# The first stage of a conv/attention block kernel: row sums of squares on TensorE, scale and shift in one turn, and another order of steps

## The chip, the cores and the metric

The kernel runs on one core of a Trainium2 chip. The metric is the device time of one execution in microseconds (us); lower is better. Every time below comes from the timed runs of the kernel before or from the trace of one profiled execution of it.

## What is computed

Two layers of a small diffusion transformer work on 256 latent tokens (`x`) and 256 context tokens (`ctx`) of width 1024, in float32. The first stage, which the change concerns, is the beginning of layer 0:

```
mod = (silu(c) @ mod_w[i] + mod_b[i]).reshape(bsz, 3, 3, 1, D_MODEL)
modc = (silu(c_ctx) @ mod_w[i] + mod_b[i]).reshape(3, 3, D_MODEL)
h = rms(x) * g * (1 + scale) + shift       # scale = mod[:,0,1], shift = mod[:,0,0]
gte, up = split(h @ w13, 2)                # FFN_HIDDEN = 2816 columns each
x = x + 0.5 * gate * ((silu(gte) * up) @ w2)
```

`rms(x)` divides each token by the root of the mean of its squares over the 1024 features. `c` (for x) and `c_ctx` (for ctx) give two sets of scale and shift. After this feed-forward part come a short convolution, a second feed-forward, grouped attention and two more feed-forwards; they are not changed.

## The kernel before, in words

**Layout.** Features lie on the 128 partitions: `x` is 128 x 8 x 512, feature tile k (0 to 7) by 512 tokens, the latent 256 first (s = 0), then the context 256 (s = 1). Weights come from HBM as float32; ScalarE rounds each to a high part (`wh`, L108), VectorE forms the rest (`wl`, L109), and a product is three matmuls: high by high, low by high, high by low. Each of these moves 512 columns. Plain float32 matmuls (those on `ones`, `ident`, `rowsum`, `sccol`) are issued as two passes each, so the trace counts two instructions for one call.

**Constants.** Five small loads go out on ScalarE's DMA queue through `cload` (L72): `ccol`, `modb`, `normg`, `ident`, `rowsum`. The four loads of `x`, 512 KB each, go out on SP's queue (L81). All later loads of the first stage go out on SP's queue in the order of the step list. In the program the DMAs of these two queues take eight completion semaphores in turn, and an issue waits until the DMA that used its semaphore eight places earlier has landed.

**The row sums.** `square_add` (L254 to L263) squares each tile of `x` on ScalarE and adds it to `acc` on VectorE. `rms_sum` (L265 to L280) then multiplies `acc` with a column of ones: for 128 tokens one matmul with `acc` as the weights and one moving column (L270), four in all; then the root on ScalarE and the reciprocal on VectorE. `rms_all` (L285 to L292) spreads the result over all partitions with `ident` (L288), and `first_inv` copies it to SBUF (`ris`, L947).

**Scale and shift.** A quarter q covers two feature tiles. `mod_load` (L907) loads 1 MB of modulation weights for the scale (ch = 1) or the shift (ch = 0). `mod_pe` (L912) multiplies them with the padded silu(c) in `sccol`, 32 columns of weights in four column groups of the array at once (L920, eight matmuls), and copies the 256 sums from PSUM to `row` (L925, ScalarE). `mod_turn` (L928) turns the row into columns with `rowsum` (L932, two matmuls) and adds the bias (L937, VectorE). Scale and shift of one quarter are two `mod_pe` and two `mod_turn`.

**The order.** Inside a `manual_schedule` block the instructions of TensorE, VectorE, ScalarE and SP are issued in the order in which the program writes them. After `fill(WARM)` (39 matmuls of `ones` by `ones` that no result uses, L891) and the sums, the string `FIRST_STEPS` is gone through: L loads modulation weights, R loads FFN weights, P is `mod_pe`, X is `first_inv`, U is `scale_q` (x times g times `ris`, L957), T is `mod_turn`, W splits a quarter of the FFN weights, F is `fill(FILL)` (5 matmuls), N is `norm_one` (the normalised tile and its low part, L967 to L981), h, w, l are the three kinds of product for one FFN column block i, quarter q and tile j, M all six of them for both tiles, S the last load. The three column blocks i = 0, 1, 2, four quarters, two tiles, three kinds and two halves (gate and up) make 144 matmuls of 512 columns (all L994). The next block, i = 3, begins at L137. After that the kernel is the same in both versions.

## Time and profile before

| | |
|---|---|
| time, median of 3 runs | 1556.71 us (1556.7 to 1556.72) |
| the profiled execution | 1558.75 us |
| its span in the trace | 1557.0 us |
| TensorE (PE) busy | 1545.5 us, 99% of the span |
| VectorE (DVE) busy | 1284.5 us, 82% |
| ScalarE (ACT) busy | 781.9 us, 50% |
| granted TensorE clock, mean | 0.999 |

In the profile PE is the matmul side of TensorE, PEld its weight loads, SPq and ACTq the DMA issues of those queues. A row of the timeline has the start, the length, the engine, the line, the operation, the tiles (out<-in), the shape, how many instructions are merged in it, and in brackets how long the engine was idle before it and what ended that. Neighbouring matmuls overlap, so the distance between their starts, and not their length, is what one costs in a row of many.

### The profile page before, as it was taken

How to read it: one execution, taken by the hardware profiler on the slowest of the kernel's cores; microseconds unless marked ns; L12 is line 12 of the kernel's file. 1: busy time of each engine (PE TensorE's matmuls, PEld its weight loads, DVE VectorE, ACT ScalarE, POOL GpSimd, SP SyncE). 2: the span in 40 equal slices, each digit the busy share in tenths (PEclk: the TensorE clock that was granted, in tenths of full speed). 3: DMA queues.
4: the chain of work that ended last, by engine and by line, in shares of the span. 5: the costliest groups of instructions: out<-in, count | busy, mean ns of one | idle time of the engine just before them, and what ended most of it. 6: DMA issues, size and time to landing. Idle time of an engine off the chain costs nothing.

```text
span 1557.0 us, 26280 instructions
## 1 busy us (share of the span) xinstructions
PE 1545.5 (99%) x10252; PEld 1416.9 (91%) x10252; DVE 1284.5 (82%) x2003; ACT 781.9 (50%) x1297; POOL 221.8 (14%) x187
## 2 busy tenths in 40 slices
PE   9999999999999999999999999999999999999999
PEld 7898998998888899989999899989999899998888
DVE  5789799799987489978979888968978888898676
ACT  5642553544322366436446476436446455774553
POOL 0012212200000012032032012022042002300000
PEclk9999999999999999999999999999999999999999
DMA  9557477475565424655656634655767843266562
GB/s 368 197 167 197 115 186 203 111 199 166 187 204 178 115 62 121 207 142 146 199 149 153 205 77 123 203 156 133 220 183 169 263 158 122 92 237 221 170 196 75
DMA packets 88254, 263.53 MB, mean 169 GB/s; under 512 B 10817, under 2 KB 12609, under 8 KB 88129
## 3 DMA queue, kind: packets, MB, share of 16 engines
q1 hardware_dynamic: 69408, 230.72, 45.7%
q0 software_dynamic: 16128, 29.37, 11.3%
q10 hardware_dynamic: 2592, 1.76, 0.4%
q8 instruction: 80, 1.31, 0.3%
q14 instruction: 46, 0.37, 0.1%
HBM read 259.45 MB, written 1.05 MB: 167 GB/s over the span
## 4 chain that ended last, share of the span: by engine, by line
PE 96%; DVE 2%; ACT 1%; DMA 1%; issue 0%; POOL 0%; ACTq 0%; DVEq 0%; POOLq 0%
PE py L138 9%; PE py L137 9%; PE py L139 9%; PE p L137 7%; PE p L139 7%; PE p L138 7%; PE q L137 5%; PE q L139 5%; PE q L138 5%; PE py L145 2%; PE pu L145 2%; PE pg L145 2%; PE py L147 1%; PE pg L147 1%; PE pu L147 1%; PE pv L137 1%
## 5 line engine op out<-in xcount | busy, mean ns | idle before, releaser
L108 ACT ACTIVATE wh<-wr 128x1024 fp32r<-128x1024 f32 (+2 forms) x446 | 394.7, 913 | 338.0 <-PE py L138 128.1
L109 DVE TENSOR_TENSOR wl<-wr,wh 128x1024 fp32r<-128x1024 f32 (+2 forms) x446 | 456.5, 1048 | 84.3 <-ACT wh L108 64.7
L178 DVE CUSTOM_DVE_ANT_0 junk<-wr,scbc,modb 128x1024 bf16<-128x1024 f32 x213 | 274.5, 1289 | 8.7 <-DMA wr<-in_modT 6.9
L138 PE MATMUL py<-gl,wh 128*128 128x512 f32 (+1 forms) x570 | 213.4, 374 | 0.0
L137 PE MATMUL py<-gh,wh 128*128 128x512 f32 (+1 forms) x570 | 213.3, 374 | 0.0
L139 PE MATMUL py<-gh,wl 128*128 128x512 f32 (+1 forms) x570 | 212.9, 373 | 0.0
L699 POOL TENSOR_SCALAR wr<-wr 128x512 f32<-128x512 f32 x56 | 101.3, 1809 | 542.4 <-DMA wr<-in_w 292.2
L562 DVE SCALAR_TENSOR_TENSOR x<-py,mod,x 128x256 f32<-128x256 f32 x213 | 94.2, 478 | 66.5 <-PE py L139 55.0
L137 PE MATMUL p<-th,wh 128*128 128x256 f32 x448 | 126.8, 283 | 0.0
L139 PE MATMUL p<-th,wl 128*128 128x256 f32 x448 | 126.8, 283 | 0.0
L138 PE MATMUL p<-tl,wh 128*128 128x256 f32 x448 | 126.8, 283 | 0.0
L139 PEld LDWEIGHTS py<-gh,wl 128*128 128x128 f32 x570 | 107.3, 188 | 19.3
L137 PEld LDWEIGHTS py<-gh,wh 128*128 128x128 f32 x570 | 107.4, 188 | 18.3
L138 PEld LDWEIGHTS py<-gl,wh 128*128 128x128 f32 x570 | 107.4, 188 | 18.0
L115 POOL DMA_DIRECT2D w4l<-in_w x56 | 54.1, 966 | 445.2 <-ACT w4l L114 423.6
L137 PE MATMUL q<-bh,wh 128*128 128x256 f32 x320 | 90.8, 284 | 0.8 <-ACT wh L108 0.8
L139 PE MATMUL q<-bh,wl 128*128 128x256 f32 x320 | 90.8, 284 | 0.0
L138 PE MATMUL q<-bl,wh 128*128 128x256 f32 x320 | 90.5, 283 | 0.0
L138 PEld LDWEIGHTS p<-tl,wh 128*128 128x128 f32 x448 | 86.0, 192 | 0.3
L137 PEld LDWEIGHTS p<-th,wh 128*128 128x128 f32 x448 | 86.0, 192 | 0.3
L139 PEld LDWEIGHTS p<-th,wl 128*128 128x128 f32 x448 | 86.0, 192 | 0.0
L759 ACT ACTIVATE sg<-sg 128x512 f32<-128x512 f32 x56 | 35.4, 632 | 90.9 <-DVE sg L758 90.6
(303 smaller groups left out, 4060.4 us busy)
## 6 DMA issues: line engine op xcount, KB each, us to landing
wr<-in_w SPq DMA_DIRECT2D x120, 512.0 KB, 4.8
wr<-in_modT SPq DMA_DIRECT2D x117, 512.0 KB, 4.7
wr<-in_w2b SPq DMA_DIRECT2D x64, 448.0 KB, 4.0
wr<-in_w2a SPq DMA_DIRECT2D x32, 512.0 KB, 4.5
wr<-in_w SPq DMA_DIRECT2D x56, 256.0 KB, 3.9
wr<-in_w POOLq DMA_DIRECT2D x56, 256.0 KB, 5.9
w4l<-in_w POOLq DMA_DIRECT2D x56, 256.0 KB, 6.0
pm<-in_mod SPq DMA_DIRECT2D x16, 512.0 KB, 10.2
```

The lines of the kernel that those rows point to most:

```text
L108: nc.scalar.activation(out=hi, in_=src, func=AF.Copy)
L109: return nc.vector.tensor_tensor(out=lo, in0=src, in1=hi.bitcast(F32), op=ALU.subtract)
L115: nc.gpsimd.dma_start(out=lo, in_=src, accum_op=ALU.add)
L137: nc.tensor.matmul(ps, wh, mh, start=first, stop=False, **kw)
L138: nc.tensor.matmul(ps, wh, ml, start=False, stop=False, **kw)
L139: nc.tensor.matmul(ps, wl, mh, start=False, stop=last, **kw)
L145: nc.tensor.matmul(ps, w[0], m[2], start=first and n == 0, stop=False)
L147: nc.tensor.matmul(ps[:, :S], w[1], m[0], start=False, stop=last and n == len(ms) - 1)
L178: nc.vector.tensor_tensor_reduce(out=junk, in0=raw, in1=scbc[:, v, :], scale=0.5 if ch in (2, 8) else 1.0, scalar=modb[:, l, col : col + 1 ...
L562: ins = nc.vector.scalar_tensor_tensor(out=x[:, m, s * S : s * S + S], in0=ps[:, o : o + S], scalar=g[:, m, s : s + 1], in1=x[:, m, s * S ...
L699: nc.gpsimd.tensor_scalar(out=r1[:, :T2], in0=r2[:, :T2], scalar1=-1.0, scalar2=None, op0=ALU.mult)
L759: nc.scalar.activation(out=self.sg, in_=self.sg, func=AF.Silu)
```

## The change

1. **Sums.** `square_add` is no longer used in this stage. `first_sums` squares the even tiles of `x` on ScalarE and the odd ones on VectorE, and multiplies each squared tile at once with a column of ones, four matmuls per tile, which add up in PSUM over the eight tiles: 32 matmuls in place of 4. `first_inv` does root, reciprocal and spreading for all four token blocks together.
2. **Turn.** The shift's matmuls add into the same PSUM rows as the scale's (`sccol` is padded so that the two land in different rows of a group of 32), so that one copy and one `mod_turn` (two matmuls with four columns, then two additions) serve both.
3. **Fills.** `WARM` goes from 39 to 30; F takes its count from the step list, which has F6 ahead of the spreading, F12 ahead of the first shift product, F4 ahead of the first turn, and F5 where F was. Together 57 in place of 44.
4. **Order.** In the later quarters, other products stand between P and T: `w100 w101 h200` in the first, `h011 w011 l011` in the second, `h211 w211 l211` in the third. Some M steps are written out as h, w, l. W of block 2's first half is cut into H (ScalarE) and D (VectorE), set apart.
5. **Second copy of a normalised tile.** `norm_one` makes it on VectorE for (q, j) = (0,0), (2,0), (3,0) and on ScalarE for the rest; before, VectorE did all of quarter 0 and every j = 0.
6. **One constant load.** The five small arrays are packed into `first` (128 x 340) and loaded by one DMA.

```diff
-WARM = 39
-FILL = 5
+WARM = 30
 FIRST_STEPS = (
-    "L10 L00 R00 R10 P10 X U0 L11 P00 L01 T10 T00 W00 N00 W01 N01 F h000 w000 l000 R20 W10 "
-    "W11 h001 w001 h100 h101 l001 l100 l101 U1 P11 L12 P01 L02 T11 T01 w100 w101 N10 N11 W20 "
-    "W21 U2 M01 R01 R11 P12 L13 P02 L03 T12 T02 M11 R21 N20 N21 W02 W03 M20 W12 W13 U3 M21 "
-    "P13 P03 T13 T03 W22 W23 M02 N30 N31 M12 M22 M03 M13 M23 S"
+    "L10 L00 R00 R10 F6 X U0 P10 L11 F12 P00 L01 F4 T0 W00 N00 W01 N01 F5 h000 w000 l000 R20 W10 "
+    "W11 h001 w001 h100 h101 l001 l100 l101 U1 H20 H21 P11 L12 P01 L02 w100 w101 h200 T1 D20 D21 "
+    "N10 N11 h201 l200 l201 w200 w201 U2 h010 w010 l010 R01 R11 P12 L13 P02 L03 h011 w011 l011 T2 "
+    "M11 R21 N20 N21 W02 W03 W12 W13 U3 h210 w210 l210 P13 P03 h211 w211 l211 T3 W22 W23 M02 "
+    "N30 N31 M12 M22 M03 M13 M23 S"
 )
-    ccol = cload("ccol", [P, KT, 2])
+    first = cload("first", [P, CUTS[-1]])
+    ccol, modb, normg, ident, rowsum = (first[:, a:b] for a, b in zip(CUTS, CUTS[1:]))
...
-    for k in range(KT):
-        square_add(k, 0, T2)
...
             nc.tensor.matmul(
-                pr[g : g + 32, :S], sccol[:, k, :], raws[k // 4][:, o : o + S],
-                start=(k < 4), stop=(k >= 4), tile_position=(0, g),
-            )
+                pr[g : g + 32, :S], sccol[:, k, c : c + 32], raws[k // 4][:, o : o + S],
+                start=(ch == 1 and k < 4), stop=(ch == 0 and k >= 4), tile_position=(0, g),
+            )
...
+    def first_sums():
+
+        pq = psmall("ss")
+        for k in range(KT):
+            sq = tp.tile([P, T2], F32, name=nm("sq"), tag="sg" if k % 2 else "gm", bufs=3)
+            if k % 2:
+                nc.vector.tensor_tensor(out=sq, in0=x[:, k, :], in1=x[:, k, :], op=ALU.mult)
+            else:
+                nc.scalar.activation(out=sq, in_=x[:, k, :], func=AF.Square)
+            for i in range(4):
+                nc.tensor.matmul(
+                    pq[:, S + i : S + i + 1], sq[:, i * P : i * P + P], ones[:, 0:1],
+                    start=(k, i) == (0, 0), stop=(k, i) == (KT - 1, 3), skip_group_check=True,
+                )
+        return pq
...
-            if q == 0 or j == 0:
+            if (q, j) in ((0, 0), (2, 0), (3, 0)):
...
         fill(WARM)
-        sums = [rms_sum(s) for s in range(2)]
+        pqs = first_sums()
```

More of the change, by code (lines that the diff above doesn't have):

```diff
@@ L27 @@
 EARLY = 4
+CUTS = (0, 16, 160, 208, 336, 340)
 HEADS = 8
@@ L75, in cload @@
         return t
-    ccol = cload("ccol", [P, KT, 2])
+    first = cload("first", [P, CUTS[-1]])
+    ccol, modb, normg, ident, rowsum = (first[:, a:b] for a, b in zip(CUTS, CUTS[1:]))
+    ccol = ccol.rearrange("p (k v) -> p k v", v=2)
+    modb = modb.rearrange("p (l c) -> p l c", l=2)
+    normg = normg.rearrange("p (l j k) -> p l j k", l=2, j=3)
     x = act.tile([P, KT, T2], F32, name="x", tag="x")
@@ L81, in hybrid_kernel @@
         nc.sync.dma_start(x[:, 2 * q : 2 * q + 2, :], a["xT"][:, 2 * q : 2 * q + 2, :])
-    modb = cload("modb", [P, 2, 72])
-    normg = cload("normg", [P, 2, 3, KT])
-    ident = cload("ident", [P, P])
     ones = const.tile([P, P], F32, name="ones", tag="ones")
@@ L92, in hybrid_kernel @@
     )
-    sccol = const.tile([P, KT, 32], F32, name="sccol", tag="sccol")
+    sccol = const.tile([P, KT, 34], F32, name="sccol", tag="sccol")
     nc.vector.memset(sccol, 0.0)
-    nc.scalar.activation(out=sccol[:, :, :2], in_=ccol, func=AF.Silu)
-    rowsum = cload("rowsum", [P, 2])
+    nc.scalar.activation(out=sccol[:, :, 2:4], in_=ccol, func=AF.Silu)
     scbc = mp.tile([P, 2, D], F32, name="scbc", tag="scbc", bufs=1)
@@ L500, in second @@
             def second():
-                z.ri = tp.tile([P, S], F32, name=nm("ris"), tag="ris0", bufs=1)
+                z.ri = tp.tile([P, T2], F32, name=nm("ris"), tag="ris", bufs=1)[:, :S]
                 nc.scalar.copy(z.ri, rms_all(*box["ri"]))
@@ L915, in mod_pe @@
         raws = rows[ch, q]
-        pr = psum("pr") if (ch, q) == (1, 0) else psmall("pr")
+        if ch:
+            rows[q] = psum("pr") if q == 0 else psmall("pr")
+        pr = rows[q]
+        c = 2 if ch else 0
         for k in range(KT):
@@ L920, in mod_pe, with mod_turn @@
             nc.tensor.matmul(
-                pr[g : g + 32, :S], sccol[:, k, :], raws[k // 4][:, o : o + S],
-                start=(k < 4), stop=(k >= 4), tile_position=(0, g),
-            )
+                pr[g : g + 32, :S], sccol[:, k, c : c + 32], raws[k // 4][:, o : o + S],
+                start=(ch == 1 and k < 4), stop=(ch == 0 and k >= 4), tile_position=(0, g),
+            )
+    def mod_turn(q):
+        pr = rows[q]
         row = tp.tile([P, T2], F32, name=nm("row"), tag="gm", bufs=3)
         nc.scalar.copy(row[:, :S], pr[:, :S])
-        rows[ch, q] = pr, row
-    def mod_turn(ch, q):
-        pr, row = rows[ch, q]
         for j in range(2):
             nc.tensor.matmul(
-                pr[:, S + 2 * j : S + 2 * j + 2], row[:, j * P : j * P + P], rowsum,
+                pr[:, S + 4 * j : S + 4 * j + 4], row[:, j * P : j * P + P], rowsum,
                 start=True, stop=True,
@@ L936, in mod_turn, with first_inv @@
         k2 = slice(2 * q, 2 * q + 2)
-        nc.vector.tensor_tensor(
-            out=(A00 if ch else B00)[:, k2, :],
-            in0=pr[:, S : S + 4].rearrange("p (k v) -> p k v", v=2),
-            in1=both(sb1[:, k2] if ch else modb[:, 0, k2]),
-            op=ALU.add,
-        )
-    def first_inv():
+        turned = pr[:, S : S + 8].rearrange("p (k c v) -> p k c v", k=2, c=2)
+        for ch in (1, 0):
+            nc.vector.tensor_tensor(
+                out=(A00 if ch else B00)[:, k2, :], in0=turned[:, :, 1 - ch, :],
+                in1=both(sb1[:, k2] if ch else modb[:, 0, k2]), op=ALU.add,
+            )
[13 more added lines that the diff above has]
+        return pq
+    def first_inv(pq):
+        rs = tp.tile([P, 4], F32, name=nm("rs"), tag="rs4", bufs=1)
+        nc.scalar.activation(
+            out=rs, in_=pq[:, S : S + 4], func=AF.Sqrt, scale=1.0 / D, bias=eps_t
+        )
+        ri = tp.tile([P, 4], F32, name=nm("ri"), tag="ri4", bufs=1)
+        nc.vector.reciprocal(ri, rs)
+        t = tp.tile([P, T2], F32, name=nm("ris"), tag="ris", bufs=1)
         for s in range(2):
-            ris.append(tp.tile([P, S], F32, name=nm("ris"), tag=f"ris{s}", bufs=1))
-            nc.scalar.copy(ris[s], rms_all(*sums[s]))
+            ris.append(t[:, s * S : s * S + S])
+            nc.scalar.copy(ris[s], rms_all(psmall("ri") if s else pq, ri[:, 2 * s : 2 * s + 2]))
     def raw_of(k, s):
@@ L1023, in first_raw, with first_w, put @@
         ws[i] = lambda o: tuple(t[:, o % T2 : o % T2 + P] for t in cut[i][o // T2])
-    def first_w(i, p):
-        j = (1, 0, 3, 2)[p]
-        o = j % 2 * T2
-        ins = split(*cut[i][j], raws[i, j // 2][:, o : o + T2])
-        rows[f"W{i}"] = ins.ins
+    def first_w(part):
+        def put(i, p):
+            j = (1, 0, 3, 2)[p]
+            o = j % 2 * T2
+            hi, lo = cut[i][j]
+            raw = raws[i, j // 2][:, o : o + T2]
+            if part != "D":
+                nc.scalar.activation(out=hi, in_=raw, func=AF.Copy)
+            if part != "H":
+                rows[f"W{i}"] = nc.vector.tensor_tensor(
+                    out=lo, in0=raw, in1=hi.bitcast(F32), op=ALU.subtract
+                ).ins
+        return put
     steps = {
@@ L1033, in hybrid_kernel @@
         "T": mod_turn,
-        "F": lambda: fill(FILL),
+        "F": lambda *n: fill(int("".join(map(str, n)))),
         "S": load_sc,
@@ L1037, in hybrid_kernel @@
         "R": first_raw,
-        "W": first_w,
-        "X": first_inv,
+        "W": first_w("W"),
+        "H": first_w("H"),
+        "D": first_w("D"),
+        "X": lambda: first_inv(pqs),
         "U": scale_q,
@@ L1419, in _layout @@
     d["c2"] = np.stack([f("c")[0], f("c_ctx")], axis=0)
-    d["ccol"] = d["c2"].reshape(2, KT, P).transpose(2, 1, 0)
+    ccol = d["c2"].reshape(2, KT, P).transpose(2, 1, 0)
     mw = f("mod_w")
@@ L1424, in _layout @@
     d["modT"] = mw.transpose(0, 2, 1).reshape(2, 36, 2, P, D).transpose(0, 1, 3, 2, 4).reshape(2, 36, P, 2048)
-    d["modb"] = f("mod_b").reshape(2, 72, P).transpose(2, 0, 1)
-    d["normg"] = f("norm_g").reshape(2, 3, KT, P).transpose(3, 0, 1, 2)
+    modb = f("mod_b").reshape(2, 72, P).transpose(2, 0, 1)
+    normg = f("norm_g").reshape(2, 3, KT, P).transpose(3, 0, 1, 2)
     w13 = f("ffn_w13").reshape(2, 2, 2, KT // 2, P, 2, NM, P)[:, :, :, :, :, ::-1]
@@ L1462, in _layout @@
     d["sinT"] = np.sin(ang).T * sign[:, None]
-    d["ident"] = np.eye(P, dtype=np.float32)
-    d["rowsum"] = (np.arange(P)[:, None] % 32 == np.arange(2)).astype(np.float32)
+    ident = np.eye(P, dtype=np.float32)
+    rowsum = (np.arange(P)[:, None] % 32 == np.arange(4)).astype(np.float32)
+    d["first"] = np.concatenate([t.reshape(P, -1) for t in (ccol, modb, normg, ident, rowsum)], axis=1)
     return {k: np.ascontiguousarray(v) for k, v in d.items()}
```

## The prediction

> **What bounds the kernel now.** I read the page first: shares by engine, then the chain that ended last.

> ```profile
> PE 1545.5 (99%) x10252; PEld 1416.9 (91%) x10252; DVE 1284.5 (82%) x2003; ACT 781.9 (50%) x1297; POOL 221.8 (14%) x187
> PE 96%; DVE 2%; ACT 1%; DMA 1%; issue 0%; POOL 0%; ACTq 0%; DVEq 0%; POOLq 0%
> ```

> TensorE (PE) is the chain from end to end. So what counts is when PE leaves the first stage (block i = 3, L137): what follows is the same code on the same engines. The windows show what PE does, and how it is clocked, in the stretches that matter.

> ```profile
> 0.70:4.10 3.40, 3.05 (x14) 3.05 (x15) 0.45 (x3) 1.28 (x1) 0.00 (x0) 1.00 0.63 170
> 4.20:7.50 3.30, 3.30 (x31) 3.30 (x31) 0.89 (x3) 2.37 (x6) 0.00 (x0) 1.00 1.02 370
> 11.00:14.30 3.30, 1.74 (x21) 1.44 (x23) 1.55 (x3) 2.70 (x5) 0.00 (x0) 1.00 1.01 390
> 14.40:17.70 3.30, 3.30 (x28) 2.08 (x20) 0.59 (x2) 0.74 (x2) 0.00 (x0) 0.50 1.04 421
> 66.00:1557.00 1491.00, 1483.28 (x9843) 1367.91 (x9841) 1241.65 (x1909) 741.52 (x1225) 221.57 (x183) 1.00 0.57 163
> 379.60:382.90 3.30, 1.87 (x15) 1.56 (x14) 2.94 (x8) 2.19 (x5) 0.00 (x0) 1.00 0.54 155
> ```

> The columns are window, length, busy time of PE, PEld, DVE, ACT and POOL, the granted clock, the DMA share and GB/s. After 66 us PE is busy 1483.28 of 1491.00, so a delay at its start isn't absorbed later. Then the timeline of the start, where the change sits.

> ```profile
> 1.05 10.42 PE L891 MATMUL idle<-ones 128*128 128x128 f32 x78 [1.05 <-DVE eps_t L88]
> 10.83 1.15 ACT L261 ACTIVATE sq<-x 128x512 f32<-128x512 f32 x2 [1.85 <-DMA x<-in_xT]
> 13.04 1.05 PE L270 MATMUL ss<-ones,acc 128*128 128x1 f32 x8 [1.56 <-DVE acc L263]
> 14.02 1.66 PE L920 MATMUL pr<-pm,sccol 128*32 128x256 f32 x16
> 15.61 2.08 PE L288 MATMUL ss<-ident,ri 128*128 128x128 f32 x8
> 17.62 1.12 PE L920 MATMUL pr<-pm,sccol 128*32 128x256 f32 x16
> 18.66 1.18 PE L932 MATMUL pr<-rowsum,row 128*128 128x2 f32 x8
> 19.95 0.16 DVE L937 TENSOR_TENSOR mod<-pr,modb 128x4 f32<-128x4 f32 x1 [0.47 <-PE pr L932]
> ...
> 20.15 1.09 ACT L967 ACTIVATE hh<-hr,mod,A 128x256 fp32r<-128x256 f32 x2 [0.43 <-DVE mod L937]
> 21.29 0.50 PE L994 MATMUL pg<-hh,wh 128*128 128x512 f32 x1 [0.23 <-ACT hh L967]
> ```

> Before, the start is paced by data: the last load of x holds ScalarE until 10.83, PE idles 1.56 us, then sums, spreading, two products and turns follow, and the first real product starts at 21.29. PE's fill ran beside this and cost nothing.

> **The price of a pass.** Of the 78 fill passes 14 lie in the slow first stretch, up to 4.1 (3.05 us). The other 64 fill 4.1 to 11.2 (the run ends at 11.47; the last length, 0.28, overhangs its slot by 0.16): 0.111 us each. The 8 one-column passes at L270 take 1.05 us with a last length of 0.25 (the group's mean, below): (1.05 - 0.25) / 7 = 0.114. A one-column pass thus costs as much as a 128-column fill.

> ```profile
> L270 PE MATMUL ss<-ones,acc 128*128 128x1 f32 x8 | 1.1, 253 | 1.6 <-DVE acc L263 1.6
> L261 ACT ACTIVATE sq<-x 128x512 f32<-128x512 f32 x7 | 4.0, 619 | 2.0 <-DMA x<-in_xT 2.0
> L263 DVE TENSOR_TENSOR acc<-acc,sq 128x512 f32<-128x512 f32 x7 | 4.8, 692 | 1.5 <-ACT sq L261 1.0
> L977 ACT ACTIVATE hr<-hr,mod,A 128x256 f32<-128x256 f32 x6 | 3.2, 587 | 0.0
> SPq L81 <- DMA ccol<-in_ccol: 2.9, 1, 2.9
> ```

> **The change, part by part: up to the first product.** The constants become one load, so the fourth load of x no longer waits for the semaphore that `ccol` held (2.9 us in the last row, the wait view of SP's queue). x should be complete near 9, two squares per load on two engines (0.62 and 0.69 us) by 10. The seven additions (4.8 us on VectorE) and the idle 1.56 us go. But the sums are now 32 calls, 64 passes, all in PE's queue behind the fill, and everything else of PE stands behind them. In PE's order, at 0.111 us a pass and the full clock:

> - fill of 30 calls: 18 passes fewer, 11.3 - 2.0 = 9.3
> - 64 sum passes, 7.1: 16.4. The squares come early enough: the seventh and eighth need the buffers of the first two, which PE frees near 10.2 and 11.1, while it wants them at 14.6 and 15.5.
> - F6, 12 passes, 1.3: 17.7. Root and reciprocal run under it.
> - spreading, 8 passes, 0.9: 18.6. At half clock it took 2.08.
> - the scale's product, 1.04 (from 17.62 to 18.66 before): 19.7
> - F12, 24 passes, 2.7: 22.4
> - the shift's product, 1.04: 23.4
> - F4, 8 passes, 0.9: 24.3. The copy of the row runs under it; so do `ris` and U0 under F12 and the products.
> - the turn, 4 passes and the last one's overhang, 0.6: 24.9
> - two additions of 0.16 with a hand-over of 0.05 each: 25.3; before, 19.95 + 0.16 = 20.11
> - from there to the first product as before, 21.29 - 20.11 = 1.18: **26.5**, that is **5.2 us late**.

> The saved wait for x is worth nothing here: PE doesn't reach the last squares until 15 us. All loads of the stage land as early or earlier, and their users come later, so no DMA wait is added. F5 (1.1 us) lies under the 1.18.

> **From the first product to block 3.** Before: 65.43 - 21.29 = 44.14 us.

> ```profile
> 26.80 0.39 PE L994 MATMUL pu<-hl,wh 128*128 128x512 f32 x1
> 27.11 1.93 PE L920 MATMUL pr<-pm,sccol 128*32 128x256 f32 x32
> 28.98 1.22 PE L932 MATMUL pr<-rowsum,row 128*128 128x2 f32 x8
> 30.06 0.48 PE L994 MATMUL pg<-hh,wl 128*128 128x512 f32 x1
> 30.38 0.40 PE L994 MATMUL pu<-hh,wl 128*128 128x512 f32 x1
> 30.61 0.40 PE L994 MATMUL pg<-hh,wl 128*128 128x512 f32 x1
> 30.85 0.39 PE L994 MATMUL pu<-hh,wl 128*128 128x512 f32 x1
> 31.65 0.50 PE L994 MATMUL pg<-hh,wh 128*128 128x512 f32 x1 [0.42 <-ACT hh L967]
> ...
> 32.46 0.39 PE L994 MATMUL pu<-hh,wl 128*128 128x512 f32 x1
> 32.77 0.50 PE L994 MATMUL pg<-hl,wh 128*128 128x512 f32 x1
> ...
> 65.20 0.39 PE L994 MATMUL pu<-hl,wh 128*128 128x512 f32 x1
> 65.43 0.39 PE L137 MATMUL pg<-hh,wh 128*128 128x512 f32 x1
> ```

> Products in a row start 0.23 us apart. In each of three later quarters the turn has 4 passes in place of 8: 0.44 less, 1.3 in all. Parting P from T adds one change of kind per quarter: 0.31 - 0.23 = 0.08 on the way in (26.80 to 27.11) and 0.32 - 0.23 = 0.09 on the way out (30.06 to 30.38): 0.5 back, a value that no row shows for these pairs. If the ways in and out cost nothing it is 0, if each costs the 0.50 that the product at 31.65 takes after a wait, six of them cost 3. I take 0.5, by the nearest rows. The two stalls after the first of these turns, 0.80 - 0.23 = 0.57 at 31.65 and some 0.2 at 32.77, go: ten products now stand between the turn and the tile that it scales. What is late next is the first column block itself: its second tile's copy moves to ScalarE (2 x 0.59), ahead of block 1's weights, and pushes `h100` by some 0.2. Sum: -1.3 + 0.5 - 0.8 + 0.2 = -1.4, so 42.7 us.

> At the full clock throughout, block 3 starts at 26.5 + 42.7 = 69.2, against 65.43: 3.77, so **+3.7**.

> **The clock.** The rows show one more price. In 11.00:14.30 PE was busy 1.74 us, about 1.0 of it one-column passes, and was granted 0.50 in the next 3.4 us. In 379.60:382.90 it was busy hardly more, 1.87, with wide products, and kept 1.00. I read that as: a one-column pass, nearly all of it a weight load, hardly counts as work to what grants the clock. After the change 9.3 to 16.4 holds nothing else. If the stretches lie as before (borders near 10.9, 14.4, 17.8 and 21.2), 10.9 to 14.4 is such work alone, the clock halves at 14.4, the rest of the sums run at half speed to about 18.4, so the next stretch is light too, and only the fills after them bring the clock back at 21.2. Half of 6.8 us is lost: 3.4. That makes 3.7 + 3.4 = **+7.1**. Bounds of this unknown: 0, if such passes count in full, and 5.1, if the borders lie so that three stretches (10.2 us) are slow.

> [...]

> **Rivals.**

> *The clock holds* (0.34). For it: PE has no idle time after the change, and the two windows compared differ little. Against: the 0.50 after 1.56 us of idle time. Time: 1556.7 + 3.7 = 1560.4.

> *Sum passes are cheaper in a long row* (0.07). The only row shows eight. Passes of L920 start 1.04 / 16 = 0.065 us apart, four at a time; so priced, the sums take 4.2, 2.9 less: 1557.5. Against: (1.05 - 0.25) / 7 is already a steady distance.

> *The start follows the data* (0.03). If a sum pass took 0.02 us, the sums would keep up with the squares, end near 10.5, and the first product would start near 20.2: -1.1 there and -1.4 after, 1554.2. It decides from 0.053 us a pass down, where 64 passes give back 3.7. [...] The trace's 0.114, with a weight load for each pass, doesn't agree.

> *Slower still* (0.06): three slow stretches, 1556.7 + 3.7 + 5.1 = 1565.5.

> **How the numbers follow.** Likeliest, at 0.50: sums bound by PE and the clock at half for two stretches, 1556.71 + 7.1 = 1563.8. The sum is made on the profiled execution (span 1557.0, its time 1558.75); a shift of its span is carried over to the median as it stands. About 0.2%, 3.1 us, is what a measurement can tell from no change; the holding clock (+3.7, give or take 0.8) straddles it a little. So slower: 0.50 + 0.06 + 0.27 = 0.83; within: 0.07 + 0.07 = 0.14; faster 0.03. The range leaves out the cheap passes and the slowest case: 1559.4 to 1564.9.

> **What would show it.** In the profile after: L955 with 64 passes from about 9.3, at 0.11 us apart, without waits for squares; a granted clock of 0.50 somewhere between 12 and 21; the first L1019 product at 26.5 (clock held) or near 30; from there 42.7 us to block 3 without the stall of 0.42 for `hh`. I am wrong if the sums wait for x, if they end before 12, or if PE waits after a turn.

## The result and the profile after

| | before | after |
|---|---|---|
| median of 6 runs each | 1556.72 us (1556.57 to 1557.06) | 1568.84 us (1564.92 to 1569.55) |
| the profiled execution | 1558.75 us | 1569.0 us |
| its span | 1557.0 us | 1567.2 us |
| first product (pg, block 0) | 21.29 us | 34.12 us |
| block i = 3 starts | 65.43 us | 75.84 us |

The change makes the kernel slower by 12.1 us: ratio 1.0068, 95% interval 1.0058 to 1.0078. The page of after, its busy times, granted clock over 40 slices, and shares of the chain that ended last:

```profile
PE 1558.0 (99%) x10318; PEld 1429.9 (91%) x10318; DVE 1280.4 (82%) x1995; ACT 781.2 (50%) x1292; POOL 221.3 (14%) x187
PEclk8999999999999999999999999999999999999999
PE 97%; DVE 2%; ACT 1%; issue 0%; POOL 0%; ACTq 0%; DVEq 0%; POOLq 0%
```

PE is still the chain. It is busy 12.5 us longer for only 66 more instructions, and the first slice of the clock now shows 8. So the time lies in the first slice. The timeline of after, PE alone, from the start to the first product:

```profile
1.04 9.40 PE L892 MATMUL idle<-ones 128*128 128x128 f32 x60 [1.04 <-DVE eps_t L90]
10.28 11.17 PE L955 MATMUL ss<-ones,sq 128*128 128x1 f32 x64
21.31 2.91 PE L892 MATMUL idle<-ones 128*128 128x128 f32 x12
24.01 1.06 PE L289 MATMUL ss<-first,ri 128*128 128x128 f32 x4
...
25.86 1.44 PE L922 MATMUL pr<-pm,sccol 128*32 128x256 f32 x16
...
32.46 1.36 PE L892 MATMUL idle<-ones 128*128 128x128 f32 x10
34.12 0.50 PE L1019 MATMUL pg<-hh,wh 128*128 128x512 f32 x1 [0.30 <-ACT hh L992]
```

After its first microsecond PE waits for nothing until the 0.30 at the very end. The sums take 11.03 us (10.28 to 21.31) for 64 passes. The windows of after (window, length, busy time of PE, PEld, DVE, ACT and POOL with their counts, granted clock, DMA share, GB/s) show why:

```profile
4.20:6.10 1.90, 1.90 (x10) 1.90 (x10) 0.37 (x2) 0.30 (x2) 0.00 (x0) 1.00 1.04 404
...
9.60:12.90 3.30, 3.30 (x33) 3.30 (x31) 0.69 (x1) 1.57 (x2) 0.00 (x0) 1.00 1.02 406
13.10:16.30 3.20, 3.20 (x17) 3.20 (x16) 0.00 (x0) 0.15 (x1) 0.00 (x0) 0.50 1.02 412
...
19.90:23.10 3.20, 3.20 (x16) 3.20 (x16) 0.18 (x1) 0.27 (x1) 0.00 (x0) 0.50 1.03 422
23.30:26.50 3.20, 3.20 (x21) 2.73 (x23) 0.61 (x2) 0.75 (x2) 0.00 (x0) 0.50 1.03 422
26.70:30.00 3.30, 3.30 (x36) 2.87 (x28) 0.94 (x3) 0.00 (x0) 0.00 (x0) 1.00 1.04 416
```

The clock is 0.50 from between 12.90 and 13.10 to between 26.50 and 26.70: 13.6 us, or four stretches of 3.4, in which a window counts 16 to 21 instructions of PE, against 33 and 36 in the two windows at full clock. The first row is a trap: its column says 1.00, but 10 passes in 1.90 us are 0.19 each, against 0.10 from 6.20 to 9.50 (32 in 3.30), so I take the clock as still half there. The column stays at 1.00 over the place near 6.2 where the passes quicken. Last, the rest of the stage, from the same timeline of PE:

```profile
39.61 0.39 PE L1019 MATMUL pu<-hl,wh 128*128 128x512 f32 x1
...
42.13 0.40 PE L1019 MATMUL pu<-hh,wl 128*128 128x512 f32 x1
...
43.05 0.39 PE L1019 MATMUL pu<-hh,wh 128*128 128x512 f32 x1
...
43.97 0.40 PE L1019 MATMUL pu<-hh,wh 128*128 128x512 f32 x1
...
75.84 0.39 PE L138 MATMUL pg<-hh,wh 128*128 128x512 f32 x1
```

From the first product to block 3 it takes 75.84 - 34.12 = 41.72 us, against 44.14: 2.42 less. So the change loses 12.83 up to the first product and wins 2.42 after it. The sum, 10.4, is the difference of the spans (10.2) within 0.2.

### The profile page after: what moved, and what is told of

Its sections match the earlier page's. It is cut to its first block, busy times and chain, and to the rows that moved or that the text cites. A ratio compares the mean times of both kernels' runs of the same rounds, so it can differ in the third digit from the quotient of the medians.

```text
span 1567.2 us, 26378 instructions
## 1 busy us (share of the span) xinstructions
PE 1558.0 (99%) x10318; PEld 1429.9 (91%) x10318; DVE 1280.4 (82%) x1995; ACT 781.2 (50%) x1292; POOL 221.3 (14%) x187
## 3 DMA queue, kind: packets, MB, share of 16 engines
HBM read 259.45 MB, written 1.05 MB: 166 GB/s over the span
## 4 chain that ended last, share of the span: by engine, by line
PE 97%; DVE 2%; ACT 1%; issue 0%; POOL 0%; ACTq 0%; DVEq 0%; POOLq 0%
PE py L139 9%; PE py L138 9%; PE py L140 9%; PE p L138 7%; PE p L140 7%; PE p L139 7%; PE q L138 5%; PE q L140 5%; PE q L139 5%; PE py L146 2%; PE pu L146 2%; PE pg L146 2%; PE py L148 1%; PE pg L148 1%; PE pu L148 1%; PE pv L138 1%
## 5 line engine op out<-in xcount | busy, mean ns | idle before, releaser
L109 ACT ACTIVATE wh<-wr 128x1024 fp32r<-128x1024 f32 (+2 forms) x434 | 388.4, 922 | 336.3 <-PE py L139 127.7
L110 DVE TENSOR_TENSOR wl<-wr,wh 128x1024 fp32r<-128x1024 f32 (+2 forms) x434 | 449.2, 1059 | 83.7 <-ACT wh L109 64.4
L179 DVE CUSTOM_DVE_ANT_0 junk<-wr,scbc,first 128x1024 bf16<-128x1024 f32 x213 | 274.3, 1288 | 7.8 <-DMA wr<-in_modT 6.0
L138 PEld LDWEIGHTS py<-gh,wh 128*128 128x128 f32 x570 | 107.4, 188 | 18.4
```

The costliest lines, as they stand in the source:

```text
L109: nc.scalar.activation(out=hi, in_=src, func=AF.Copy)
L110: return nc.vector.tensor_tensor(out=lo, in0=src, in1=hi.bitcast(F32), op=ALU.subtract)
L138: nc.tensor.matmul(ps, wh, mh, start=first, stop=False, **kw)
L179: nc.vector.tensor_tensor_reduce(out=junk, in0=raw, in1=scbc[:, v, :], scale=0.5 if ch in (2, 8) else 1.0, scalar=modb[:, l, col : col + 1 ...
```

## Theories, and the experiments

**The theory.** The loss is the row sums. A pass that moves one column costs as much as one that moves 128 against weights of the same size (in before 0.114 us and 0.111), and, as I read the 0.50 behind a row of such passes, they hardly count as work to what grants the clock, so the clock halves too. (A wide pass, below, is one that moves 128 columns or more; a narrow one moves a single column.) **Rivals:** the sums wait for their squares or for x; the added fills are the loss; the clock depends on something else than the kind of pass; and, for the gain of 2.42, that the joint turn brings it without the order, or the order without it. The first rival falls by the timeline of after, where the seventh and eighth squares (the fourth on each engine) wait for PE, and not PE for them:

```profile
11.31 0.63 ACT L953 ACTIVATE sq<-x 128x512 f32<-128x512 f32 x1 [2.22 <-PE ss L955]
12.16 0.69 DVE L951 TENSOR_TENSOR sq<-x 128x512 f32<-128x512 f32 x1 [3.00 <-PE ss L955]
```

The kernel before was run beside each group: medians 1556.80 (17 runs), 1557.03 (17) and 1557.10 (15).

### Everything but the sums

After, with the sums of before, WARM 39 and no F6, F12, F4:

```diff
-WARM = 30
+WARM = 39
...
-    "L10 L00 R00 R10 F6 X U0 P10 L11 F12 P00 L01 F4 T0 W00 N00 W01 N01 F5 h000 w000 l000 R20 W10 "
+    "L10 L00 R00 R10 P10 X U0 L11 P00 L01 T0 W00 N00 W01 N01 F5 h000 w000 l000 R20 W10 "
...
-        pqs = first_sums()
+        pqs = [rms_sum(s) for s in range(2)]
```

> The changed kernel with the row sums of before (squares on ScalarE, additions on VectorE, 4 matmuls for the sums), the fill of 39 ahead of them and no F6, F12, F4; the joint turn, the order, the one constant load stay. Theory (one-column passes hold TensorE's queue and count too little for its clock): first product at 20.5 to 21.3, then 41.7 us to block 3 as in the changed kernel, so 1554 to 1555, 2 to 3 us under the kernel before. Rival (the turn or the order itself cost time at the start): first product after 24, 1558 or more.

Measured: 1554.12 us (10 runs), ratio 0.9981 (0.9971 to 0.9990), as expected, though the first product comes 1.1 us earlier than that. The timeline of PE in this kernel:

```profile
19.36 0.49 PE L999 MATMUL pg<-hh,wh 128*128 128x512 f32 x1 [0.30 <-ACT hh L972]
...
61.13 0.39 PE L138 MATMUL pg<-hh,wh 128*128 128x512 f32 x1
```

Block 3 follows after 41.77 us, so the stage behind takes as long as in after. The change without its sums is faster than before by 2.7 us; the sums with their fills cost the other 14.7. The two profiles are 4.3 apart at block 3 (65.43 and 61.13), because before's has a slow stretch, 14.40:17.70, that costs it 1.7 and that this one hasn't.

### Only the fills out

```diff
-    "L10 L00 R00 R10 F6 X U0 P10 L11 F12 P00 L01 F4 T0 W00 N00 W01 N01 F5 h000 w000 l000 R20 W10 "
+    "L10 L00 R00 R10 X U0 P10 L11 P00 L01 T0 W00 N00 W01 N01 F5 h000 w000 l000 R20 W10 "
```

> The changed kernel without F6, F12 and F4 (44 passes that no result uses). Theory: the sums still run at half clock to about 21.3; F6 saves 2.0 of its 2.7 (root and reciprocal need 0.7), F12 2.7, F4 0.45 of 0.9: 5.1 less, but spreading and the two products then fall into the half clock and cost about 2 more: 1563.7 to 1566. Rival A (the fills lie beside other work): 1568 to 1569. Rival B (without them the clock stays down into the products): 1569 or more, granted clock 0.50 beyond 27 us.

Measured: 1564.57 us (1560.79 to 1564.96, 4 runs), 1.0043 (1.0028 to 1.0058). The windows of this kernel show the half clock in one row; behind it, the sums from its timeline of PE:

```profile
12.20:25.70 13.50, 12.93 (x68) 11.73 (x71) 2.06 (x6) 1.63 (x4) 0.00 (x0) 0.50 1.03 416
```

```profile
9.85 11.60 PE L955 MATMUL ss<-ones,sq 128*128 128x1 f32 x64
```

The fills cost 4.3 of the 12.1 us, near their 44 passes at 0.111 (4.9). They neither cause the half clock nor prevent it: it lasts four stretches without them too. The last stretch at full clock (3.4 us, up to 12.1) still had fill until 9.85, about 34% of it, and the clock fell all the same.

### The kind of pass: 3 fills behind each tile, and 1

The first kernel puts `fill(3)` behind each tile's four sums, 48 passes more than after; the second `fill(1)`, 16 more. Nothing else differs.

```diff
                     start=(k, i) == (0, 0), stop=(k, i) == (KT - 1, 3), skip_group_check=True,
                 )
+            fill(3)
```

> The changed kernel with three fill calls (6 passes) after the four sums (8 passes) of each tile: 48 passes more for TensorE. Theory (the clock counts what streams through the array): with 43% wide passes the clock stays 1.00 after the start; 112 passes of 0.111 end near 22 to 23, all after them is at full clock, first product near 32 to 33, 1566.5 to 1568: not slower than the changed kernel for all the added work. Rival (only the number of passes counts, the clock falls as before): 48 passes add 5 to 10 us, 1574 to 1579.

> The changed kernel with one fill call (2 passes) after the four sums (8 passes) of each tile, so 20% wide passes in place of 43%. If a share of 20% is enough to hold the clock: 32 passes fewer than with three fills, 3.6 us less, first product near 29.2, 1563.5 to 1564.2. If it is not: granted clock 0.50 from about 13 to 27 or later, 1567 to 1572.

Measured with three: 1567.41 us (1567.11 to 1567.51, 4 runs), 1.0066 (1.0051 to 1.0081). With one: 1571.66 (1568.55 to 1572.35, 4 runs; the profiled execution is the fastest), 1.0093 (1.0078 to 1.0109). The windows with three, then those with one, then the timeline of PE with one:

```profile
9.40:12.70 3.30, 3.30 (x32) 3.30 (x32) 0.14 (x1) 1.64 (x2) 0.00 (x0) 1.00 1.03 403
...
16.20:19.50 3.30, 3.30 (x32) 3.30 (x32) 0.00 (x0) 0.00 (x0) 0.00 (x0) 1.00 1.01 410
```

```profile
11.90:15.30 3.40, 3.40 (x32) 3.40 (x32) 0.67 (x1) 0.84 (x1) 0.00 (x0) 1.00 1.03 412
15.40:18.70 3.30, 3.30 (x19) 3.30 (x17) 0.00 (x0) 0.00 (x0) 0.00 (x0) 0.50 1.01 407
```

```profile
14.24 0.95 PE L955 MATMUL ss<-ones,sq 128*128 128x1 f32 x8
15.05 0.50 PE L892 MATMUL idle<-ones 128*128 128x128 f32 x2
15.36 1.70 PE L955 MATMUL ss<-ones,sq 128*128 128x1 f32 x8
16.92 0.78 PE L892 MATMUL idle<-ones 128*128 128x128 f32 x2
```

PE is busy all the time in both. With 6 wide passes to 8 narrow ones (43%) the clock holds, and 48 passes more are no slower than after. With 2 to 8 (20%) it falls. So in these two kernels the kind of pass decides (1.00 and 0.50 in the windows from 15.4 on), not idle time and not the count. The last rows price it: eight narrow passes take 15.05 - 14.24 = 0.81 us at full clock and 16.92 - 15.36 = 1.56 at half, so such a pass takes about twice as long when the clock is at half.

### The sums the other way round

Here `ones` are the weights and the squared tile moves, 512 columns at a time: 8 calls, and the result already lies on all partitions, so the spreading goes (root and reciprocal work on 128x512).

```diff
-            for i in range(4):
-                nc.tensor.matmul(
-                    pq[:, S + i : S + i + 1], sq[:, i * P : i * P + P], ones[:, 0:1],
...
+            nc.tensor.matmul(pq, ones, sq, start=k == 0, stop=k == KT - 1)
```

> The changed kernel with the operands of the sums turned round: ones (128 x 128) are the weights and the squared tile moves, 512 columns, 8 matmuls (16 passes); the sum then stands on all partitions, so that the spreading matmuls go, and root and reciprocal work on 128 x 512. By the fill's rate a pass takes 0.43, 6.8 us in all, as much as 64 one-column passes at full clock. Theory: clock 1.00 throughout after the start, first product near 26, 1560 to 1561.5. Rival (the clock falls whatever the passes are, or the time was that of the passes alone): granted clock 0.50 again, 1566 or more.

Measured: 1561.18 us (8 runs), 1.0025 (1.0014 to 1.0036). The windows of this kernel, then its timeline of PE:

```profile
10.80:17.60 6.80, 6.80 (x18) 3.02 (x17) 0.69 (x1) 1.91 (x2) 0.00 (x0) 1.00 1.02 397
```

```profile
10.78 7.03 PE L954 MATMUL ss<-sq,ones 128*128 128x512 f32 x16
...
26.97 0.50 PE L1010 MATMUL pg<-hh,wh 128*128 128x512 f32 x1 [0.30 <-ACT hh L983]
```

The sums take the 7 us that 64 narrow passes would take at full clock, and now the clock holds. This is the prediction's first rival, made on purpose. First product at 26.97, where the prediction's sum at full clock had 26.5 (the fill ends 1.5 later than in that sum, and the spreading, 0.9, is gone). Against after it is 1568.84 - 1561.18 = 7.7 us. In the two profiles the first product comes 34.12 - 26.97 = 7.15 earlier; 0.9 of that is the spreading, and the fill ends 0.5 later, so about 6.75 is the clock's, and half of 13.6 is 6.8.

### The sums alone

The kernel before with only `first_sums` and the new `first_inv`, WARM 30, and before's order, turn and loads:

```diff
-WARM = 39
+WARM = 30
...
-        sums = [rms_sum(s) for s in range(2)]
+        pqs = first_sums()
```

> The kernel before with the new sums alone (32 one-column matmuls, squares on two engines, the fill of 30), its own order, five constant loads and separate turns. Theory: the sums end near 21 at half clock, the spreading and the products after them at half too; first product at 28 to 30, then 44.1 us as before: 1562 to 1566. Rival (it is the added fills, the order or the joint turn that cost): within 1.5 us of the kernel before.

Measured: 1568.22 us (1565.99 to 1571.48, 4 runs), 1.0072 (1.0058 to 1.0086): a miss of 2 us above the expected range. The windows of its profiled execution, the slowest of the four:

```profile
30.30:33.60 3.30, 3.30 (x17) 3.30 (x17) 2.15 (x7) 2.22 (x5) 0.00 (x0) 0.50 1.04 415
33.80:37.00 3.20, 3.20 (x9) 2.35 (x9) 3.20 (x9) 1.54 (x4) 0.00 (x0) 0.50 1.03 410
37.20:40.00 2.80, 2.80 (x16) 2.01 (x19) 1.42 (x4) 0.00 (x0) 0.00 (x0) 1.00 1.04 414
```

Here the clock was at half from 13.2 to 37.1, seven stretches; the one from 30.3, with the end of the turn and then fills, didn't raise it, and even products ran at half speed (9 in 3.20 us, 0.43 apart in place of 0.23). Behind one stretch of products alone (33.80:37.00) it was 1.00 again. So the sums alone, in before's order, cost 11.2 us (1568.22 against 1557.03), and how long the half clock lasts hangs on what follows them. The profiled execution has one more loss that after hasn't: at 25.66 PE has waited 2.34 us for the reciprocal. In before's order the copy of the row stands ahead of the root on ScalarE, which is busy 1.92 us with three instructions from 22.20 to 25.50; the table load ahead of the root takes 1.28 us in the traces of before and after.

### The joint turn in the old order

The first kernel of this section, with the step order and second copies of before, two turns made one:

```diff
...
-    "W11 h001 w001 h100 h101 l001 l100 l101 U1 H20 H21 P11 L12 P01 L02 w100 w101 h200 T1 D20 D21 "
+    "W11 h001 w001 h100 h101 l001 l100 l101 U1 P11 L12 P01 L02 T1 w100 w101 N10 N11 W20 "
...
-            if (q, j) in ((0, 0), (2, 0), (3, 0)):
+            if q == 0 or j == 0:
```

> The joint turn and the one constant load with the row sums and the order of before (no products between P and T; the second copies on the engines of before). Theory: of the 2.4 us that the changed kernel gains between its first product and block 3, 3 times 4 passes, 1.3 to 1.8, are the turn's, and the stalls of 0.8 stay: first product near 19.4, 42.3 to 42.8 to block 3, 1554.7 to 1555.3. Rival (the gain is the order's): 44 us to block 3, 1556 or more.

Measured: 1556.69 us (11 runs), 0.9997 (0.9988 to 1.0005): a miss, and the rival is right. The timeline of PE:

```profile
20.84 0.49 PE L998 MATMUL pg<-hh,wh 128*128 128x512 f32 x1 [0.30 <-ACT hh L971]
...
26.31 0.39 PE L998 MATMUL pu<-hl,wh 128*128 128x512 f32 x1
...
29.11 0.61 PE L934 MATMUL pr<-first,row 128*128 128x4 f32 x4 [0.55 <-ACT row L932]
29.58 0.48 PE L998 MATMUL pg<-hh,wl 128*128 128x512 f32 x1
29.89 0.40 PE L998 MATMUL pu<-hh,wl 128*128 128x512 f32 x1
...
65.00 0.39 PE L137 MATMUL pg<-hh,wh 128*128 128x512 f32 x1
```

From the first product to block 3 it takes 65.00 - 20.84 = 44.16 us, as before the change (44.14). From the product ahead of the pair to the second behind it: 29.89 - 26.31 = 3.58, exactly before's 30.38 - 26.80. Of the 8 turn passes 4 are gone, and PE waits 0.55 for the copy of the row in their place. Before, the shift's product and the first turn hid that copy. In after the products put between P and T hide it, and the same stretch takes 42.13 - 39.61 = 2.52 and 43.97 - 43.05 = 0.92 with six products in between; less four product slots of 0.23, that is 2.52, where before's 3.58 less two slots is 3.12. So 0.60 in this quarter. The joint turn wins it only with the new order; what the new order wins without the joint turn was not run.

### Less fill ahead of the sums

```diff
-WARM = 30
+WARM = 14
```

> The changed kernel with a fill of 14 in place of 30 ahead of the sums, nothing else. Theory: the sums start near 6.5 but run at half clock for the greater part, end between 16 and 20, and the clock comes back only with F6 and after; first product at 27 to 32, 1562 to 1567. Rival (the sums were only queued behind too long a fill): they end near 13.6, first product near 23.7, 1558 to 1559.

Measured: 1563.70 us (1563.35 to 1565.34, 4 runs), 1.0041 (1.0025 to 1.0056). The windows of this kernel, then its timeline of PE:

```profile
16.60:19.90 3.30, 3.30 (x17) 3.30 (x17) 0.18 (x1) 0.26 (x1) 0.00 (x0) 0.50 1.02 395
20.00:23.30 3.30, 3.30 (x23) 2.51 (x25) 1.13 (x3) 0.75 (x2) 0.00 (x0) 0.50 1.03 423
```

```profile
17.59 2.91 PE L892 MATMUL idle<-ones 128*128 128x128 f32 x12
```

The 16 calls taken away ahead of the sums are 32 passes, 3.6 us at 0.111; the time falls by 5.1 against after by the medians, and by 3.7 between the two profiled executions (1569.0 and 1565.34), so the rest lies within the spread of single executions (after's own runs lie 4.6 apart). PE's queue, and not the data, sets the start. The half clock again lasts four stretches, 9.7 to 23.4: in the one from 16.5 to 19.9 the fills have PE from 17.59 on, 69% of it, and the clock doesn't rise at its end.

### Five loads in place of one

After, with before's five constant loads:

```diff
-    first = cload("first", [P, CUTS[-1]])
...
+    ccol = cload("ccol", [P, KT, 2])
...
+    modb = cload("modb", [P, 2, 72])
+    normg = cload("normg", [P, 2, 3, KT])
+    ident = cload("ident", [P, P])
...
```

> The changed kernel with the five small constant loads of before in place of the one. Theory (TensorE is the bound of the start, the loads are not): x is complete near 10.8 instead of 9.7, the sums need its last tile after 17; no change, 1565 to 1569.6 as the changed kernel, first product 30.5 to 34.5. Rival (the loads still pace the start): about 1 us more on top.

Measured: 1567.47 us (1566.19, 1568.76, 1568.80, 1565.35), 1.0063 (1.0050 to 1.0077): no change against after, as expected. Its profiled execution, 1566.19, is the case that I had predicted, two slow stretches; its windows and its timeline of PE:

```profile
14.70:18.00 3.30, 3.30 (x18) 3.30 (x17) 0.00 (x0) 0.00 (x0) 0.00 (x0) 0.50 1.01 410
18.10:21.40 3.30, 3.30 (x17) 3.30 (x17) 0.18 (x1) 0.26 (x1) 0.00 (x0) 0.50 1.02 418
21.50:24.80 3.30, 3.30 (x37) 2.60 (x36) 1.73 (x4) 0.75 (x2) 0.00 (x0) 1.00 1.03 422
```

```profile
18.20 2.91 PE L893 MATMUL idle<-ones 128*128 128x128 f32 x12
...
30.07 0.50 PE L1020 MATMUL pg<-hh,wh 128*128 128x512 f32 x1 [0.30 <-ACT hh L993]
```

Here the fills begin at 18.20, hardly behind a border, fill the stretch, and the clock rises at its end. In after they began at 21.31, in the middle of one (57% of it), and it took another.

### A version that beats both

The sums with `ones` as the weights, squares and ones written in the products' type, one pass per tile (x1 in the rows below); `fill(1)` behind each; WARM 14; F4, F5 and F2 in place of F6, F12 and F4. The second kernel is the same with five loads.

```diff
-WARM = 30
+WARM = 14
...
-    "L10 L00 R00 R10 F6 X U0 P10 L11 F12 P00 L01 F4 T0 W00 N00 W01 N01 F5 h000 w000 l000 R20 W10 "
+    "L10 L00 R00 R10 X U0 F4 P10 L11 F5 P00 L01 F2 T0 W00 N00 W01 N01 F5 h000 w000 l000 R20 W10 "
...
-            sq = tp.tile([P, T2], F32, name=nm("sq"), tag="sg" if k % 2 else "gm", bufs=3)
+            sq = tp.tile([P, T2], F32R, name=nm("sq"), tag="sg" if k % 2 else "gm", bufs=3)
...
+            nc.tensor.matmul(pq, ones_r, sq, start=k == 0, stop=k == KT - 1)
+            fill(1)
```

> A version meant to be the fastest: the changed kernel with ones as the weights of the sums and the squared tile moving, rounded to the type of the products (one pass of 0.23 instead of two of 0.43), one fill call after each tile, a fill of 14 ahead, F4 and F5 round the scale's product, F2 ahead of the turn. Theory: the sums follow the loads of x and end near 11 to 11.5, clock 1.00 from its first rise on, the first product waits for the shift's weights (landing near 14.7) and starts at 18.6 to 19.4, 1553 to 1554.2. Rival (a shorter fill leaves the clock at half): first product after 21, 1556 or more.

> The fastest version so far (wide rounded sums, fill of 14) with the five small loads. Theory (here the loads pace the start): x complete near 10.8 instead of 9.7 and the shift's weights near 15.9 instead of 14.7, first product 18.9 to 19.6 instead of 18.15: 1553.6 to 1554.4. Rival (the loads are hidden here too): 1552.8 to 1553.1.

Measured: 1552.89 us (7 runs), 0.9971 (0.9960 to 0.9982), a little better than expected, and with five loads 1554.10 (11 runs), 0.9980 (0.9972 to 0.9989). The timeline of PE with one load, then with five:

```profile
10.48 0.48 PE L957 MATMUL ss<-sq,ones_r 128*128 128x512 f32 x1
...
18.15 0.51 PE L1014 MATMUL pg<-hh,wh 128*128 128x512 f32 x1 [0.39 <-ACT hh L987]
```

```profile
10.82 0.50 PE L958 MATMUL ss<-sq,ones_r 128*128 128x512 f32 x1 [1.21 <-ACT sq L957]
...
18.98 0.50 PE L1015 MATMUL pg<-hh,wh 128*128 128x512 f32 x1 [0.39 <-ACT hh L988]
```

Now the sums follow the squares, and the one load is worth 1.2 us by the medians: with five, PE waits 1.21 for the square of the last load of x, and the first product comes 0.83 later (the other 0.4 has no row here). In after the same load was worth nothing that the runs show.

## Why the prediction was wrong

**Direction, and the mechanism: right.** The sums are bound by PE's queue, the squares are never waited for, the clock halves in a row of one-column passes, and the one load is worth nothing here. The terms that add up to 26.5 hold where the clock does.

**The step that failed: the length of the half clock.** The prediction put it as "only the fills after them bring the clock back at 21.2", two stretches, 3.4 us. It was four, 13.6 us (13.0 to 26.6, where the prediction had 14.4 to 21.2), 6.8 lost. Its reading of one light stretch was that the next heavy one ends the half clock. In the runs, at half clock, a stretch with 57% wide passes (after) and one with 69% (WARM 14) didn't end it, and one with some 96% (five loads) did. And the borders aren't where they were in before's profile: there the clock first rose near 4.1, in after near 6.2. They differ from execution to execution, so that after has no single time: two of its six runs, 1564.92 and 1565.59, lie 3.9 and 3.3 below the median, a mean clock of 0.998 beside 0.995 or 0.996. By that clock they should be executions with two stretches, as the profiled one with five loads is (1566.19, 0.998); they weren't profiled. My upper bound of three stretches for this cost (5.1) was too low, and no row excluded four.

In these profiles the half clock lasts one or more times 3.4 us: once in before (14.4 to 17.8), twice with five loads (14.6 to 21.4), four times in after (13.6 us), seven times with the sums alone (13.2 to 37.1). Its first rise lies between 4.1 and 7.2 us. The prediction carried the borders of one profile over, where they should have stood as unknown. And idle time of PE isn't what brought the clock down in after: it has none between 2 and 33 us.

**A second term, 2 us: the execution that the sum was made on.** "A shift of its span is carried over to the median as it stands" fails, since the profiled execution of before had a slow stretch of its own (14.40:17.70, quoted in the prediction), which its usual execution, by its mean clock, lacks. Of the 49 runs of before beside the experiments, 38 have a mean clock of 1.000 and lie at 1556.07 to 1557.66; the 11 with 0.999 lie at 1558.12 to 1559.33, and the profiled one, 1558.75 at 0.999, belongs to these; the others were not profiled. That is 2.0 us between the two, which the median doesn't hold and the prediction gave back. Both numbers stood in the prediction (1556.71 and 1558.75) beside a row with 0.50, and weren't put together.

**First rise.** The fill ended at 10.28, not at 9.3: 1.0 us, because the clock rose 2 us later than in before's profile.

**The rest of the stage.** Forecast -1.4, measured -2.4. The turns won 0.60 in the first of the three quarters and 0.55 in each of the others, 1.7, where the forecast had 1.3 less 0.5 for changes of kind; the other 0.7 is the stalls', where it had 0.8 less 0.2. The attribution was wrong too: I gave the 1.3 to four passes fewer, and without the new order they are worth nothing (3.58 us both times).

Together: 5.2 + 1.0 + 6.8 = 13.0 up to the first product (12.83 measured), -2.4 after it, +10.4 on the span; the two profiled executions are 1569.0 - 1558.75 = 10.2 apart, and 2.0 more against before's median, 12.3 (12.1 by both medians).

**The rivals.** The clock that holds was a real case, but needs other passes (1561.18). Cheaper passes and the start that follows the data didn't occur; the best version makes the latter true. No run shows the 0.02 us a pass that the prediction tried for it: eight one-column passes took 0.81 at full clock, 0.10 each.

**Shares or counts.** In shares falling and rising differ: at full clock the clock held with 43% wide passes (three fills) and fell with 34% (only the fills out); at half clock it stayed down with 69% (WARM 14) and rose with some 96% (five loads). But at half clock a stretch holds half as many passes, and in counts the two meet. Too few were some 10 wide passes in 3.4 us (only the fills out, at full clock) and some 11 (WARM 14, at half clock); enough were some 13 (three fills, at full clock) and some 15 (five loads, at half clock). So a single number between 11 and 13 wide passes per stretch, my estimate, fits these four profiles, and they show no difference between falling and rising. It does not fit the sums alone: from 26.90 to 30.20 at half clock PE has some 19 wide passes (3 of L288, 16 of L918, these with weights of 32 columns), and in the next stretch the clock was still 0.50. No run was made to test it.

What stays open: whether such a count or something else is what decides, and what sets the borders.

## What to carry to other kernels

Price a matmul with few moving columns no lower than one with 128 and the same weights (here 0.10 to 0.114 us a pass, and 0.111), and let the data move against fixed weights where the result allows it (here 1561.18 us against 1568.84). At the start of a kernel ask of each 3.4 us how much wide matmul work is in it: in after being busy wasn't enough to hold the clock (0.50 from 13 to 26.6 us), and once lost it didn't return behind a stretch with 57% (after) or 69% (WARM 14) of such work and did behind one with some 96% (five loads). Before a profiled execution serves as the base of a sum, hold its time and its clock against the timed runs; an odd stretch in it isn't part of the median.
